# Two searches instead of one: where blocks 6 and 7 of the indexer are scored and selected

## The chip, the cores and the metric

The kernel runs on one core of one Trainium2 chip. The metric is the device time of one execution in microseconds (us). The engines are called PE (TensorE), DVE (VectorE), ACT (ScalarE), POOL (GpSimd) and SP (SyncE, which here issues all the DMAs). Each engine takes its instructions in order; between engines, semaphores make them wait.

## What is computed

A trunk of two layers over 1024 tokens of width 1024. Layer 0 has sparse latent attention whose keys are chosen by an indexer, layer 1 has windowed attention; both read a memory by cross-attention, and both end in a gated MLP with a causal convolution. The change touches the indexer of layer 0, which for every block of 128 queries scores all earlier keys and keeps the best 256:

```python
def one_block(args):
    ql, qr, qi, wi, t = args
    dots = jnp.einsum('bqhd,bsd->bqhs', qi, k_idx).astype(jnp.float32)
    score = jnp.einsum('bqhs,bqh->bqs', jax.nn.relu(dots), wi.astype(jnp.float32))
    score = jnp.where((key_pos[None, :] <= t[:, None])[None], score, -jnp.inf)
    _, idx = lax.top_k(score, topk)          # topk = 256
    c_sel = jax.vmap(lambda c, i: c[i])(c_kv, idx)
    ...                                      # softmax attention over the selected keys
    return jnp.einsum('bqhk,bqkr->bqhr', p, c_sel.astype(jnp.float32))
x = x + jnp.concatenate([mix, mem_o], axis=-1) @ w_out
x = x + conv_glu_ffn(rmsnorm(x, g_ffn[i]), f_w_up[i], f_conv_w[i], f_conv_b[i], f_w_down[i])
```

The indexer has 16 heads of width 64. Blocks 0 and 1 see at most 256 keys and need no selection.

## The kernel before

**Tiling.** The 1024 tokens are two halves of 512 and eight blocks of 128. A float32 product is made of three matmuls of high and low parts (`mm3`, lines 256 to 258); the high part of a weight is cast by ACT (line 99), its low part subtracted by POOL (line 279). PSUM holds four one-bank tiles (`pB`) and two two-bank tiles (`pS`). Nearly all else is in one pool of 51 tiles in SBUF (`t` in the rows).

**Order.** The program is written out by hand: PE's main stream calls `tick(ns)` after each few matmuls, and `tick` advances a planner's clock and the generators in `self.bg`. A generator yields the ns that its last step is meant to take, and goes on when its clock (the planner's times its rate) has caught up. So the rate and the yielded numbers set between which main instructions a background step is put, on every engine, and nothing else: matmuls of a background step don't advance the clock. `finish_bg` puts all that is left of a generator at one place.

**Stages of layer 0.** Projections; from 401 us the attention of the first half (`run_a(0)`), from 541 us its MLP (`ffn`), then attention and MLP of the second half. In the MLP, each of 22 hidden units has two projections of 24 matmuls into `pB` tiles; `conv` (lines 797 to 812) takes the first: DVE L801, ACT L802, DVE L803 and L804, ACT's Silu L810, POOL L811; then `gate` (DVE L816, ACT L820) takes the second. After each pair of units a down product makes four `pS` tiles of 12 matmuls, and each is added to the residual by DVE (L867).

**Scoring** (`indexer`, lines 1196 to 1227): a head of a block is four matmuls (L1214) into two `pB` tiles, two Relus on ACT (L1217) and a weighted add to the block's scores on DVE (L1222; the first head is L1220). Blocks 4 to 7 are 64 heads, scored during the projections at rate 0.65.

**Search** (`topk`, lines 1229 to 1322): the 256th best score of each query is found bit by bit, 32 bits. For blocks given in `act` ACT counts (a Sign with a running sum, L1274), for the others DVE counts (L1254); a step of two small DVE instructions (L1265, L1267) then sets the next bit. After the bits, blocks counted by ACT need a selection between two candidates (L1295 to L1304), and every block gets five passes that turn its scores into a mask (L1313 to L1321). Blocks 2 and 3 have a search of their own. Blocks 4 to 7 share one: DVE counts 4 and 5, ACT counts 6 and 7, and a bit is four yields of 2400 ns. It is the background entry `late`, at rate 1.0 in the first attention, 0 in its last products, 1.056 in the MLP. The masks of blocks 4 to 7 are first needed by the attention of the second half. The cross-attention of the memory for the second half (`memory()`: L713, then L752) starts when `late` is done.

Of the kernel before, what the change touches and what calls it, by code (L numbers as in the profile page):

```python
# [173 lines left out]
class Trunk:  # L174
# [1543 lines left out]
    def run(self):  # L1718
# [31 lines left out]
        def first_norms():  # L1750
            yield from self.scale_later(acc, rb, wait=8500)
            yield from self.norm_apply(rb[0], x0, g[:, 0], 2, h0, 1500)

        bn = self.add_bg(first_norms())
# [17 lines left out]
        def memory():  # L1772
            yield from self.mem_norm()
            yield from self.mem_kv(0)
            del self.mn

        self.a_qidx(0, h0, tabs[1])
        self.finish_bg(bn)
        bm = self.add_bg(memory(), 0.62)
        tabs = self.load_table("small", 1), self.load_table("q16", 1)  # L1780

        def index():
            yield 12864
            yield from self.indexer((2, 3))
            bt.append(self.add_bg(self.topk((2, 3), 1400, (3,))))
            while "qi1" not in self.marks:
                yield 500
            yield 9000
            be[1] = 0.65
            yield from self.indexer((4, 5, 6, 7))  # L1790
            late.append(self.add_bg(self.topk((4, 5, 6, 7), 2400, (6, 7))))

        late = []
        bt = []
        be = self.add_bg(index(), 1.0)
        self.finish_bg(b1)
        del x1
# [12 lines left out]
        late = late[0]  # L1810
# [7 lines left out]
        late[1] = 1.0  # L1818
        mem_o = mem[1]

        def topk_on():
            late[1] = 1.056
            yield 0

        for hf in range(2):
            x = self.load_x(a["x"][hf])
            sqs, h, hook = self.prepare(x, g[:, 3])
            last = self.run_a(hf, att, x, mem_o, bm, hook)
            late[1] = 0.0
            self.every(last)  # L1830
            rb = []
            bn = self.add_bg(self.chain([lambda: self.scale_of(sqs, rb, 1000), topk_on]))
            acc, hook = self.squares(x)
            if hf == 0:
                mem = self.mem_units(1)

                def memory():
                    while late in self.bg:
                        yield 1000
                    self.load_qmem(1)  # L1840
                    yield 9000
                    yield from self.whole(mem[0], 2200)

                def then():
                    nonlocal att
                    att = self.attn_a(1)
                    bt.append(self.add_bg(self.spread(self.chain([lambda: iter([4000]), lambda: self.begin_a(att)]), 2950)))

                bm, bt = self.add_bg(memory()), []
            else:  # L1850
                hB0 = []

                def norm0():
                    yield 55000
                    x0 = self.load_x(self.x_d[0])
                    yield from self.norm(x0, g[:, 1], hB0, 5000, 6000, 4000, True)

                b0 = self.add_bg(norm0())

                def mem_kv():  # L1860
                    yield 120000
                    yield from self.mem_norm()
                    yield 3000
                    yield from self.mem_kv(1)
                    del self.mn

                bt = [self.add_bg(mem_kv(), 0.8)]
            self.ffn(0, [(hf, x, h, rb, hook)], then=then if hf == 0 else None)
            self.finish_bg(bn, late, *bt)
            if hf == 0:  # L1870
                self.add_bg(self.store_x(x, self.x_d[0]))
                mem_o = mem[1]
# [284 lines left out]
```

## Time and profile before

| | us |
|---|---|
| median of 3 runs (2631.11 to 2632.77) | 2632.64 |
| the profiled execution | 2624.22 |
| its span | 2622.4 |
| PE busy | 2457.8 (94%) |
| DVE busy | 1708.0 (65%) |
| POOL busy | 1387.8 (53%) |
| ACT busy | 1207.9 (46%) |

A busy time is the time in which the engine has an instruction at work; a full PE can still be slow, since its granted clock (PEclk, a share of full speed) falls. The averages mix stages with different limits, so the rows below go by stretches of the span.

### The profile page before, as it was taken

The numbers are of one execution on the slowest core, as the hardware profiler recorded it, in microseconds if no ns is written. First come the engines' busy times: TensorE is split into PE (matmuls) and PEld (weight loads), VectorE is DVE, ScalarE is ACT, GpSimd is POOL, SyncE is SP. The second block draws the span as 40 slices with busy tenths as digits, with TensorE's granted clock in tenths as the row PEclk, the third lists the DMA queues.
The fourth block names the chain that finished last, engine by engine and source line by source line (L and its number), as shares of the span: only waits on it lengthen the run. The fifth ranks groups of instructions, "written<-read, shape, count | busy, mean of one in ns | idle before, by whom it ended". The sixth has DMA issues, their size and how long they took to land. (4 is left out here: it accounts for less than half of the span.)

```text
span 2622.4 us, 34006 instructions
## 1 busy us (share of the span) xinstructions
PE 2457.8 (94%) x11912; PEld 2053.0 (78%) x11912; DVE 1708.0 (65%) x2961; ACT 1207.9 (46%) x2270; POOL 1387.8 (53%) x1241
## 2 busy tenths in 40 slices
PE   7789978989998999999999989999989999999997
PEld 5678856878886888877888878878767888888886
DVE  7787788877688466665653353498786556564446
ACT  5355666655542555433333334588644444442003
POOL 5644223456665633365766665566656666664204
PEclk9899999999998999999999999999989999999999
DMA  5453343423322343322333345642254232348401
GB/s 202 148 172 120 127 159 135 149 78 97 98 87 91 126 155 107 113 97 82 105 127 97 99 115 187 213 139 88 81 193 137 104 122 97 123 170 329 142 16 65
DMA packets 121083, 333.83 MB, mean 127 GB/s; under 512 B 13008, under 2 KB 29904, under 8 KB 120912
## 3 DMA queue, kind: packets, MB, share of 16 engines
q1 hardware_dynamic: 120912, 331.66, 37.4%
q8 instruction: 94, 1.54, 0.2%
q14 instruction: 77, 0.63, 0.1%
HBM read 258.21 MB, written 73.40 MB: 126 GB/s over the span
## 5 line engine op out<-in xcount | busy, mean ns | idle before, releaser
L279 POOL TENSOR_TENSOR t<-t,t 128x512 fp32r<-128x512 f32 x829 | 1108.2, 1368 | 681.0 <-ACT t L99 273.6
L256 PE MATMUL pB<-t,t 128*128 128x512 f32 (+3 forms) x1824 | 682.1, 374 | 11.9 <-DVE t L781 4.1
L257 PE MATMUL pB<-t,t 128*128 128x512 f32 (+3 forms) x1824 | 678.8, 372 | 5.0 <-DVE t L461 2.4
L258 PE MATMUL pB<-t,t 128*128 128x512 f32 (+3 forms) x1824 | 678.3, 372 | 5.4 <-POOL t L279 5.4
L256 PE MATMUL pS<-t,t 128*128 128x512 f32 (+1 forms) x1460 | 573.8, 393 | 40.0 <-ACT t L99 19.1
L258 PE MATMUL pS<-t,t 128*128 128x512 f32 (+1 forms) x1460 | 568.5, 389 | 8.0 <-POOL t L279 7.8
L257 PE MATMUL pS<-t,t 128*128 128x512 f32 (+1 forms) x1460 | 568.0, 389 | 2.1 <-DVE t L512 2.1
L256 PEld LDWEIGHTS pB<-t,t 128*128 128x128 f32 (+1 forms) x1824 | 346.2, 190 | 72.8 <-DVE t L781 4.7
L258 PEld LDWEIGHTS pB<-t,t 128*128 128x128 f32 (+1 forms) x1824 | 345.9, 190 | 66.7 <-POOL t L279 6.7
L257 PEld LDWEIGHTS pB<-t,t 128*128 128x128 f32 (+1 forms) x1824 | 346.2, 190 | 64.7 <-DVE t L461 3.3
L256 PEld LDWEIGHTS pS<-t,t 128*128 128x128 f32 x1460 | 281.7, 193 | 100.4 <-ACT t L99 22.8
L99 ACT CAST t<-t 128x1024 fp32r<-128x1024 f32 x284 | 288.0, 1043 | 101.5 <-PE pS L258 44.1
L258 PEld LDWEIGHTS pS<-t,t 128*128 128x128 f32 x1460 | 281.0, 192 | 67.4 <-POOL t L279 12.1
L257 PEld LDWEIGHTS pS<-t,t 128*128 128x128 f32 x1460 | 281.8, 193 | 53.2 <-DVE t L512 2.5
L265 DVE TENSOR_TENSOR t<-pB,t 128x512 fp32r<-128x512 f32 (+3 forms) x248 | 149.8, 623 | 85.3 <-ACT t L264 82.7
L264 ACT CAST t<-pB 128x512 fp32r<-128x512 f32 (+3 forms) x248 | 125.7, 534 | 158.1 <-PE pB L258 96.2
L1055 DVE TENSOR_TENSOR t<-t,pS 128x1024 f32<-128x1024 f32 (+1 forms) x92 | 107.9, 1174 | 125.6 <-PE pS L258 125.5
L811 POOL TENSOR_TENSOR t<-t,t 128x512 f32<-128x512 f32 x44 | 57.5, 1306 | 161.6 <-ACT t L810 161.6
L867 DVE TENSOR_TENSOR t<-t,pS 128x1024 f32<-128x1024 f32 x88 | 106.8, 1217 | 53.0 <-PE pS L258 52.7
L1274 ACT ACTIVATE sign<-t,ti 128x1024 bf16<-128x1024 f32 (+1 forms) x96 | 96.5, 1005 | 60.5 <-DVE ti L1267 49.1
L1447 POOL TENSOR_SCALAR t<-t,st 128x128 f32<-128x128 f32 (+3 forms) x64 | 47.9, 750 | 141.3 <-DVE st L1446 88.0
L1222 DVE SCALAR_TENSOR_TENSOR t<-t,wtok,t 128x384 f32<-128x384 f32 (+5 forms) x90 | 97.0, 1077 | 24.5 <-ACT t L1217 20.7
(228 smaller groups left out, 3027.6 us busy)
## 6 DMA issues: line engine op xcount, KB each, us to landing
t<-in_up SPq DMA_DIRECT2D x138, 512.0 KB
t<-in_down SPq DMA_DIRECT2D x66, 512.0 KB
G_d<-t SPq DMA_DIRECT2D x44, 512.0 KB
t<-G_d SPq DMA_DIRECT2D x44, 512.0 KB
t<-in_a_in SPq DMA_DIRECT2D x34, 512.0 KB
t<-in_b_in SPq DMA_DIRECT2D x28, 512.0 KB
t<-in_a_out SPq DMA_DIRECT2D x20, 512.0 KB
t<-x_d SPq DMA_DIRECT2D x20, 512.0 KB
```

What stands on the lines that cost most here:

```text
L99: nc.scalar.copy(hi[:, :w], raw[:, :w])
L256: mm(out, a[0], b[0], start=start, stop=False, skip_group_check=again)
L257: mm(out, a[0], b[1], start=False, stop=False, skip_group_check=again)
L258: mm(out, a[1], b[0], start=False, stop=stop, skip_group_check=again)
L264: nc.scalar.copy(hi, src)
L265: nc.vector.tensor_tensor(lo, src, hi.bitcast(F32), op=OP.subtract)
L279: self.nc.gpsimd.tensor_tensor(lo[:, s], src[:, s], hi[:, s].bitcast(F32), op=OP.subtract)
L811: nc.gpsimd.tensor_tensor(v, v, rb[0], op=OP.mult)
L867: nc.vector.tensor_tensor(x[dp][:, :, t], x[dp][:, :, t], S, op=OP.add)
L1055: nc.vector.tensor_tensor(xp, xp, S, op=OP.add)
L1222: nc.vector.scalar_tensor_tensor(work[:, :n], tmp[:, :n], wv, work[:, :n], op0=OP.mult, op1=OP.add)
L1274: nc.scalar.activation(hits("sign")[:, :wide], self.work[blks[i]][:, :wide], AF.Sign, bias=cand[:, i:i + 1].bitcast(F32), accum_out=cnt[:, ...
```

## The change

The shared search of blocks 4 to 7 becomes two. During the projections only blocks 4 and 5 are scored, and their search (all counts on DVE, three yields of 2400 ns for a bit) starts when that is done. When the MLP of the first half has its norm, this search's rate becomes 0.8, and a new background entry starts: `later()` scores blocks 6 and 7 at rate 0.4 and then searches them at rate 1.0, all counts on ACT, three yields of 1650 ns for a bit. The cross-attention of the memory waits for both, and `finish_bg` at the MLP's end takes both.

```diff
--- before.py
+++ after.py
@@ -1787,8 +1787,8 @@
                 yield 500
             yield 9000
             be[1] = 0.65
-            yield from self.indexer((4, 5, 6, 7))
-            late.append(self.add_bg(self.topk((4, 5, 6, 7), 2400, (6, 7))))
+            yield from self.indexer((4, 5))
+            late.append(self.add_bg(self.topk((4, 5), 2400)))
 
         late = []
         bt = []
@@ -1818,9 +1818,18 @@
         late[1] = 1.0
         mem_o = mem[1]
 
+        def later():
+            yield from self.indexer((6, 7))
+            lates[1][1] = 1.0
+            yield from self.topk((6, 7), 1650, (6, 7))
+
         def topk_on():
-            late[1] = 1.056
+            late[1] = 0.8
+            if len(lates) == 1:
+                lates.append(self.add_bg(later(), 0.4))
             yield 0
+
+        lates = [late]
 
         for hf in range(2):
             x = self.load_x(a["x"][hf])
@@ -1835,7 +1844,7 @@
                 mem = self.mem_units(1)
 
                 def memory():
-                    while late in self.bg:
+                    while len(lates) < 2 or any(b in self.bg for b in lates):
                         yield 1000
                     self.load_qmem(1)
                     yield 9000
@@ -1866,7 +1875,7 @@
 
                 bt = [self.add_bg(mem_kv(), 0.8)]
             self.ffn(0, [(hf, x, h, rb, hook)], then=then if hf == 0 else None)
-            self.finish_bg(bn, late, *bt)
+            self.finish_bg(bn, *lates, *bt)
             if hf == 0:
                 self.add_bg(self.store_x(x, self.x_d[0]))
                 mem_o = mem[1]
```

PE during the projections (`pS` tiles of the queries' projection, `pB` of the scores; the tile numbers name t_2448, the index queries). One piece of the difference:

```order
 L257 MATMUL pS<-t_441,t_2241 128x512
 L258 MATMUL pS<-t_439,t_2242 128x512
-L1214 MATMUL pB<-t_834,t_2448 128x512
-L1214 MATMUL pB<-t_834,t_2448 128x384
-L1214 MATMUL pB<-t_835,t_2448 128x512
-L1214 MATMUL pB<-t_835,t_2448 128x384
 L256 MATMUL pS<-t_443,t_2241 128x512
 L257 MATMUL pS<-t_445,t_2241 128x512
```

One head of block 6, four matmuls, has left this place; 32 such heads do.

ACT at the sixth unit of the first half's MLP, before (t_2634 and t_3029 are the scores of blocks 6 and 7):

```order
L99 CAST t_5780<-t_5647 128x1024
L802 ACTIVATE t_5785<-t_5785,conv 128x512
L806 COPY prev_a<-t_5785 128x2
L810 ACTIVATE t_5785<-t_5785 128x512
L1274 ACTIVATE sign,tc<-t_2634,ti 128x1024
L820 CAST t_5736<-t_5785 128x512
L99 CAST t_5829<-t_5689 128x1024
L99 CAST t_5836<-t_5740 128x1024
L1274 ACTIVATE sign,tc<-t_3029,ti 128x1024
L1274 ACTIVATE sign,tc<-t_2634,ti 128x1024
L1274 ACTIVATE sign,tc<-t_3029,ti 128x1024
L99 CAST t_5915<-t_5778 128x1024
```

And the same place now (t_5585, t_5625 and the like at L1217 are each the Relu output of one head):

```order
L99 CAST t_5599<-t_5422 128x1024
L802 ACTIVATE t_5604<-t_5604,conv 128x512
L806 COPY prev_a<-t_5604 128x2
L810 ACTIVATE t_5604<-t_5604 128x512
L1217 ACTIVATE t_5625<-pB 128x512 x2
L1217 ACTIVATE t_5655<-pB 128x512 x2
L820 CAST t_5537<-t_5604 128x512
L99 CAST t_5664<-t_5468 128x1024
L99 CAST t_5671<-t_5541 128x1024
L1217 ACTIVATE t_5697<-pB 128x512 x2
L1217 ACTIVATE t_5723<-pB 128x512 x2
L1217 ACTIVATE t_5749<-pB 128x512 x2
```

The signs are gone from here, and two Relus of each head have come, in pairs, directly behind the unit's Silu (L810) and its cast (L820).

DVE from the sixteenth unit of the MLP into the down product behind it, before (t_3567 and the others at L867 are the residual):

```order
L816 TENSOR_TENSOR t_7095<-t_7095,pB 128x512
L1297 ISA t_7118,tc<-t_7118,t_3029 128x1024
L1297 ISA tc 128x1
L867 TENSOR_TENSOR t_3567<-t_3567,pS 128x1024
L1301 TENSOR_SCALAR ti<-tc 128x1
L1302 TENSOR_TENSOR ti<-tc 128x1
L1303 TENSOR_TENSOR ti<-ti 128x1
L1304 TENSOR_TENSOR ti<-ti,tc 128x1
L1254 TENSOR_SCALAR hit,tc<-t_3029,ti 128x1024
L867 TENSOR_TENSOR t_3569<-t_3569,pS 128x1024
L1308 TENSOR_SCALAR tc<-tc 128x4
L1313 TENSOR_SCALAR t_7194<-t_1911,ti 128x640
```

DVE from the twentieth unit into the down product behind it, now (t_5020 and t_5519 are the scores of blocks 6 and 7):

```order
L1254 TENSOR_SCALAR hit,tc<-t_5519,ti 128x1024
L1308 TENSOR_SCALAR tc<-tc 128x2
L1313 TENSOR_SCALAR t_7598<-t_5020,ti 128x896
L1315 SCALAR_TENSOR_TENSOR t_7599<-t_7598 128x896
L1317 SCALAR_TENSOR_TENSOR t_7599<-t_7599,tc,t_7598 128x896
L816 TENSOR_TENSOR t_7568<-t_7568,pB 128x512
L1319 SCALAR_TENSOR_TENSOR t_5020<-t_5020,ti,t_7599 128x896
L867 TENSOR_TENSOR t_3257<-t_3257,pS 128x1024
L1321 TENSOR_SCALAR t_5020<-t_5020 128x896
L1313 TENSOR_SCALAR t_7649<-t_5519,ti 128x1024
L1315 SCALAR_TENSOR_TENSOR t_7650<-t_7649 128x1024
L867 TENSOR_TENSOR t_3259<-t_3259,pS 128x1024
```

The end of the search of blocks 6 and 7 has moved by four units, the passes of blocks 4 and 5 are no longer in it, and passes of 6 and 7 stand ahead of the first residual add.

## Rows read from the trace of the kernel before

**Rows 1.** Busy time by stretch: us, busy time (instructions) of each engine, PEclk, DMA share, GB/s
```profile
200.00:340.00 140.00, 139.44 (x658) 115.80 (x657) 107.93 (x216) 85.19 (x187) 38.48 (x30) 1.00 0.37 120
...
340.00:363.00 23.00, 20.82 (x92) 14.80 (x90) 19.50 (x25) 15.14 (x27) 6.45 (x7) 1.00 0.53 166
...
378.00:401.00 23.00, 0.34 (x1) 0.34 (x2) 21.48 (x58) 5.70 (x15) 2.93 (x2) 0.55 0.36 129
...
401.00:430.00 29.00, 23.76 (x155) 20.09 (x155) 21.25 (x57) 20.32 (x51) 7.31 (x13) 0.94 0.21 77
...
430.00:530.00 100.00, 100.00 (x572) 86.37 (x572) 85.48 (x215) 67.10 (x139) 43.35 (x48) 1.00 0.48 159
...
566.00:602.00 36.00, 33.48 (x142) 27.30 (x141) 27.93 (x43) 20.70 (x32) 26.21 (x21) 0.95 0.27 88
...
602.00:765.00 163.00, 163.00 (x719) 134.66 (x718) 117.11 (x197) 87.63 (x134) 103.17 (x81) 1.00 0.29 97
...
765.00:850.00 85.00, 73.07 (x301) 58.17 (x301) 71.53 (x75) 23.30 (x37) 47.60 (x36) 0.90 0.24 81
```

**Rows 2.** Timeline of PE, last heads of scoring: start, us, instructions, idle before
```profile
347.35 1.20 PE L1214 MATMUL pB<-t,t 128*128 128x512 f32 x4 [0.23 <-ACT t L1217]
348.77 1.20 PE L1214 MATMUL pB<-t,t 128*128 128x512 f32 x4 [0.22 <-ACT t L1217]
```

**Rows 3.** Waits of PE, 400 to 530 us: us in total, times, longest
```profile
PE pB L713 <- DVE t L265: 22.8, 1, 22.8
```

**Rows 4.** Groups by shape, ACT, 602 to 765 us: busy us, mean ns, idle before
```profile
L1274 ACT ACTIVATE sign<-t,ti 128x1024 bf16<-128x1024 f32 x32 | 36.6, 1144 | 17.5 <-DVE ti L1267 17.2
...
L810 ACT ACTIVATE t<-t 128x512 f32<-128x512 f32 x10 | 6.3, 633 | 20.0 <-DVE ti L1265 12.4 <-DVE t L804 7.6
...
L1274 ACT ACTIVATION_READ_ACCUMULATOR sign<-t,ti 128x1 f32 x32 | 6.0, 187 | 0.0
```

**Rows 5.** Groups by shape, DVE, 602 to 765 us
```profile
L1267 DVE SCALAR_TENSOR_TENSOR ti<-ti 128x2 int32<-128x2 int32 x33 | 18.8, 569 | 1.1
...
L1265 DVE TENSOR_SCALAR ti<-tc 128x2 int32<-128x2 f32 x33 | 13.2, 400 | 0.1
```

**Rows 6.** Groups by shape, DVE, 200 to 345 us: scoring adds
```profile
L1222 DVE SCALAR_TENSOR_TENSOR t<-t,wtok,t 128x896 f32<-128x896 f32 x15 | 18.0, 1198 | 6.8 <-ACT t L1217 6.7
...
L1222 DVE SCALAR_TENSOR_TENSOR t<-t,wtok,t 128x1024 f32<-128x1024 f32 x7 | 9.0, 1283 | 5.4 <-ACT t L1217 5.4
```

**Rows 7.** Groups by shape, POOL, 602 to 765 us
```profile
L279 POOL TENSOR_TENSOR t<-t,t 128x512 fp32r<-128x512 f32 x71 | 90.6, 1310 | 31.6 <-ACT t L820 15.4 <-issue 11.5 <-ACT t L99 3.5
```

**Rows 8.** Timeline of DVE, 570 to 600 us
```profile
580.37 1.90 DVE L803 SCALAR_TENSOR_TENSOR t<-t,conv 128x511 f32<-128x511 f32 x1 [2.76 <-ACT t L802]
...
582.30 1.66 DVE L804 SCALAR_TENSOR_TENSOR t<-t,conv 128x510 f32<-128x510 f32 x1
...
587.89 1.22 DVE L867 TENSOR_TENSOR t<-t,pS 128x1024 f32<-128x1024 f32 x1
```

**Rows 9.** Timeline of DVE, 740 to 848 us
```profile
745.14 0.75 DVE L803 SCALAR_TENSOR_TENSOR t<-t,conv 128x511 f32<-128x511 f32 x1 [0.95 <-ACT t L802]
...
765.26 0.69 DVE L801 TENSOR_TENSOR t<-pB,t 128x512 f32<-128x512 f32 x1 [0.92 <-PE pB L258]
...
789.60 1.22 DVE L867 TENSOR_TENSOR t<-t,pS 128x1024 f32<-128x1024 f32 x1
...
818.07 2.07 DVE L1319 SCALAR_TENSOR_TENSOR t<-t,ti,t 128x896 f32<-128x896 f32 x1
...
821.98 2.28 DVE L1315 TENSOR_TENSOR_SCAN t<-t 128x1024 f32<-128x1024 f32 x1
```

**Rows 10.** Waits of PE, 545 to 765 us
```profile
PE pS L256 <- DVE t L867: 2.5, 1, 2.5
```

**Rows 11.** Waits of PE, 765 to 945 us
```profile
PE pS L258 <- POOL t L279: 5.3, 2, 3.1
...
PE pS L256 <- DVE ti L1301: 3.9, 1, 3.9
```

## The prediction

> **What bounds the kernel now.** I first read the busy time of every engine by stretch [rows 1], then the waits of PE, then the order in which instructions stand. PE is full wherever the change takes work from or brings work to: 139.4 of 140 us in the stretch of projections at 200 to 340 us, 100 of 100 at 430 to 530 (first attention), 163 of 163 at 602 to 765 (the first half's MLP) [rows 1]. No matmul is removed, so only idle time of PE and its slow matmuls can be won or lost. Between 340 and 850 us they lie in these places: 2.2 us at 340 to 363, the block at 378 to 401 in which PE does next to nothing, 5.2 us at 401 to 430, 2.5 us at 566 to 602 and 11.9 us at 765 to 850, with PEclk down to 0.55, 0.95 and 0.90 [rows 1]. The last one costs more than its idle time: at the 0.227 us per matmul of 602 to 765 (163 us, 719 of them) its 301 matmuls need 68.2 of 85 us, so 16.8 us are lost there.
>
> **The change, part by part**, against the profiled run (2624.2 us; the median of the runs is 8.4 us above it, so I add the difference to the median).
>
> Scoring blocks 6 and 7 is 32 heads of four matmuls, two Relus on ACT and one scaled add on DVE. Four matmuls take 4 x 0.227 = 0.91 us of a busy PE, so 29 us leave a full stretch and return in another full stretch: 0. What was wasted around them is won: the last seven heads stood alone, 1.42 us from start to start (347.35 to 348.77) instead of 0.91 [rows 2]. The whole idle time there is 2.2 us [rows 1]; I take **-2** (0 to -4).
>
> The block at 378 to 401 is PE waiting once, 22.8 us, for DVE to finish the search of blocks 2 and 3 [rows 3]. By the order the same nine counts, twelve steps and the tail of that search stand there afterwards: **0** (-2 to +2).
>
> In the first attention the search of 4 and 5 now counts two blocks every 7200 ns of the planner's clock, not every 9600, and the signs of 6 and 7 are gone from ACT. DVE is at 85.5 of 100 us there and PE is full [rows 1], so there is no stall to win but the 5.2 us at 401 to 430, where the memory attention's second part runs: **-1** (-5 to +4).
>
> The scoring in the MLP is the largest term. The stretch at 602 to 765 holds ten units (the ten Silus, L810) [rows 4], so a pair with its down product is 32.6 us, with 23.4 us of DVE. By the order one head comes to every 13 other matmuls, so 11 to a pair: 32.6 + 11 x 0.91 = 42.6 us. DVE has one step less for each bit (0.40 + 0.57 us [rows 5], 3.2 bits to a pair: -3.1) and 11 adds of 1.20 to 1.28 us, as they took during the projections [rows 6]: 23.4 - 3.1 + 13.6 = 33.9 us, 80% against 72% before. But the adds move beside a busy POOL (103 of 163 us, in pieces of 1.31 us [rows 1, 7]; 38.5 of 140 before [rows 1]). The conv's adds, which read two tiles in SBUF as these do, show what that does: the same L803 took 0.75 us at 745 us and 1.90 at 580 [rows 8, 9]. At 0.4 us more for each, DVE is at 38.3 of 42.6 us, 90%. The trace shows what follows from crowding: at 580 to 584 two such adds ran 1.90 and 1.66 us, the residual add L867 came at 587.89, and PE waited 2.5 us for it [rows 8, 10] and then ran at a lower clock (0.95 over 566 to 602 [rows 1]), about 3 us in all. ACT adds to it: a Relu stands behind the Silu, which waits for DVE, and the next head but one wants the Relu's PSUM bank; DVE's add waits for the Relu, and L867 stands behind that. Three down products fall into the scoring. The old stall of 3 us is in the first of them, so it goes (**-3**); against it I set somewhat less than one such stall for each, **+7**. Below, the adds hide at 80% of DVE (0); above, two stalls for each (+18).
>
> A rule of the Trainium skill bears on this. SBUF — State Buffer, section "Who interferes with whom": VectorE and GpSimd share a pair of ports, and a VectorE instruction with two SBUF inputs is blocked for the whole of a GpSimd instruction that reads SBUF. That speaks against moving these adds under the MLP's POOL work; the two L803 agree with it, and no row shows it for the scoring adds yet. By it each add could lose up to a whole 1.31 us, and if it did not hold for them the +7 would be about +2.
>
> Then the search of 6 and 7: 4950 ns of the planner's clock for a bit, where it was 9600 at rate 1.056. The 32 signs at 602 to 765 are 3.2 bits to a pair [rows 4]; now 5.9. ACT: 17.5 us a pair [rows 1] + 2.7 x 2 x (1.144 + 0.187) = 24.7 of 32.6. ACT takes its work in order, so waits count too: 2.0 us before each Silu and 1.1 us before the first sign of each bit, for DVE's step (20.0 us for ten, 17.5 for 16) [rows 4]. That is 4.0 + 6.5 more: 35.2 us, 2.6 over a pair, 14 us over the 5.4 pairs. Much of it falls together when ACT runs late, and at 54% of ACT nothing stalled. Where ACT is late, DVE's step waits for the sign and L867 stands behind it. I take **+4** (0 to +14).
>
> The end of the searches is all DVE: selections (L1295 to L1304), then five passes for each block. In the old place PE waited 3.9 us at the selection and 5.3 at the passes [rows 11] and lost 16.8 in all. It is now in two pieces. Blocks 4 and 5: ten passes beside one down product, some 1.4 us too much for each of two residual adds; about +3. Blocks 6 and 7: before, 24.3 us passed from the conv (L801) to the first residual add (L867) [rows 9]. By the order block 6's selection and a count (7.6 us) now stand ahead of that conv, while block 7's small steps, a count and block 6's passes (11.1 us) come before the add: 27.9 us, by the 56 rows from 765.26 to 818.07, of which the first and the last stand in [rows 9]. So PE waits some 3.6 us longer at that add, and passes such as the 2.28 us scan behind it [rows 9] crowd three more adds, about 5 us; but the four tails' 5.3 us of waiting are gone, and some of the slow matmuls behind them. Together **+2** (-8 to +8).
>
> The second memory attention waits for both searches; its second part goes from the MLP into the second attention. The same part cost up to 5.2 us in the first attention [rows 1] and about nothing in the MLP: **+2** (-1 to +5).
>
> Sum: -2 - 1 - 3 + 7 + 4 + 2 + 2 = **+9 us**, 2641.6.
>
> **The rivals.** (a) Faster: scoring hides as the counts did at 602 to 765, and two shorter ends overload DVE less than one long one, since four PSUM banks and two residual tiles each time absorb a few us. Then -2 - 1 - 3 + 1 + 0 - 7 + 0 = -12: 2621. For it: PE held 163 of 163 with DVE at 72%. Against: 80 to 90% is more, and DVE's work in the tail is the same. It decides whether DVE keeps L867 within a PSUM tile's 2.7 us. (b) Even: +4 for the scoring, +1 for the search, 0 for the tail, +1 for the memory, less 6: 2633. (c) Much slower: ACT is the bound of the dense search, in order behind DVE: +14 there and +14 in the scoring, +4 for the rest, less 6: 2659. (d) The search doesn't end before the MLP does and drains with PE idle. By the order it ends some 260 matmuls ahead, so this can hardly be; it would be slower too.
>
> **How the numbers follow.** Forecast 0.36 (2638 to 2650), (a) 0.19, (b) 0.27, (c) 0.16, (d) 0.02. A measurement of this kernel tells 0.2% apart, 5.3 us: faster (under 2627.4) is (a), 0.19; same is (b), 0.27; slower is the rest, 0.54. For 8 in 10 the range takes in most of (a) and (c): 2622 to 2662.
>
> **What would show it.** Right: in the profile after, PE waits on L867 and on the Relus' banks in the scoring stretch, at DVE 85% or more and adds of 1.5 us; waits of DVE for signs; the block at 378 us, about 29 us earlier, unchanged. The forecast is wrong if PE is full through the scoring and the dense search, or if the two ends together lose clearly less than 16.8 us.

## The result

The changed kernel takes **2669.51 us** (median of four runs, 2667.5 to 2673.6) against 2631.88 us for the kernel before on the same chip: 1.0156 times, 95% interval 1.0140 to 1.0171. It is slower by 1.6%, 37.6 us. The forecast was 2641.6 us with a range up to 2662: the direction was right, the size was not, and the time lies above the range. The profiled execution took 2670.62 us, with a span of 2668.4 us.

**Where the time went.** First the line of busy times of both pages, before and then after:

```profile
PE 2457.8 (94%) x11912; PEld 2053.0 (78%) x11912; DVE 1708.0 (65%) x2961; ACT 1207.9 (46%) x2270; POOL 1387.8 (53%) x1241
```
```profile
PE 2474.6 (93%) x11912; PEld 2067.4 (77%) x11912; DVE 1708.2 (64%) x2963; ACT 1205.2 (45%) x2266; POOL 1392.7 (52%) x1241
```

The same 11912 matmuls keep PE busy 16.8 us longer: slower matmuls, since the granted clock fell (mean PEclk 0.973 before, 0.964 after). The span is 46.0 us longer, so the other 29.2 us are idle time of PE. DVE, ACT and POOL do what they did. So the change made no work; it made PE wait, and clock was lost with the waits.

Next the stretches of the kernel after, in the columns of [rows 1]: the block at the end of the search of 2 and 3, the first attention, the scoring of blocks 6 and 7, their search, and the end of that search.

```profile
344.00:368.00 24.00, 1.38 (x7) 0.90 (x6) 21.70 (x61) 6.50 (x15) 2.93 (x2) 0.58 0.48 177
395.00:500.00 105.00, 104.45 (x593) 90.04 (x592) 93.03 (x223) 53.60 (x113) 43.97 (x49) 1.00 0.48 160
514.00:683.00 169.00, 150.37 (x629) 122.02 (x628) 116.36 (x156) 76.91 (x130) 79.29 (x57) 0.94 0.25 75
683.00:880.00 197.00, 176.17 (x734) 142.64 (x733) 105.92 (x151) 119.18 (x187) 107.07 (x82) 0.94 0.24 78
880.00:921.00 41.00, 33.56 (x137) 26.80 (x136) 37.55 (x42) 9.99 (x14) 26.69 (x16) 0.92 0.31 100
```

Where PE held 163 of 163 us before [rows 1], it now holds 150.4 of 169 and 176.2 of 197, at 0.94 of the clock. And no other engine is full in these two: DVE stands at 69% and 54%, ACT at 46% and 60%. That is the main thing to see: **no engine is full by its busy time, and yet PE waits.**

Between the same instructions in both traces, after less before: from the start of the kernel to the end of the first attention -34.3 us, of which 29.1 are the scoring that left the projections; from there to the MLP's first conv -0.9; then to the conv at which scoring ends 169.5 us for 118.1, **+22.3** over the 29.1 that came; from there to the conv at which the search ends 196.3 for 183.0, **+13.3**, though the kernel before lost its 16.8 us of [rows 1] inside that stretch; the rest of the MLP +0.5; the second attention 194.3 for 184.0, +10.3; and -0.5 up to the second MLP's down products. That is 39.8. The last 6.2 us come in code that the change doesn't touch, and the profiled run of before was 8 us under its median; I don't put them down to the change.

The waits of PE in the scoring (510 to 680 us), then in the search (680 to 935 us), in the columns of [rows 3]:

```profile
PE pS L256 <- DVE t L867: 11.4, 3, 7.5
PE pB L1214 <- ACT t L1217: 7.2, 5, 2.7
```
```profile
PE pS L256 <- DVE t L867: 28.3, 9, 6.2
```

Before, the residual add L867 was waited for once in 220 us [rows 10]. Now it is the thing most waited for. Why it is late stands in DVE's groups by shape, first in the scoring, then (L1265) in the search; the last column is the idle time ahead of the instruction and who ended it:

```profile
L1222 DVE SCALAR_TENSOR_TENSOR t<-t,wtok,t 128x1024 f32<-128x1024 f32 x15 | 23.4, 1557 | 20.7 <-ACT t L1217 20.7
L1222 DVE SCALAR_TENSOR_TENSOR t<-t,wtok,t 128x896 f32<-128x896 f32 x15 | 22.0, 1470 | 13.3 <-ACT t L1217 13.3
```
```profile
L1265 DVE TENSOR_SCALAR ti<-tc 128x2 int32<-128x2 f32 x31 | 12.2, 394 | 41.4 <-ACT sign L1274 41.4
```

DVE stands idle for 34 us in front of scoring adds, for the Relu, and for 41 us in front of search steps, for the sign. Before, the step waited 0.1 us in all [rows 5].

The longest stall, 7.5 us, shows the chain. ACT, then DVE, then PE, each a timeline (start, us, instruction, idle before):

```profile
660.68 0.62 ACT L820 CAST t<-t 128x512 fp32r<-128x512 f32 x1 [3.04 <-DVE t L816]
661.20 1.99 ACT L99 CAST t<-t 128x1024 fp32r<-128x1024 f32 x2
663.10 1.07 ACT L1217 ACTIVATE t<-pB 128x512 f32<-128x512 f32 x2
```
```profile
659.97 0.68 DVE L816 TENSOR_TENSOR t<-t,pB 128x512 f32<-128x512 f32 x1
664.21 1.98 DVE L1222 SCALAR_TENSOR_TENSOR t<-t,wtok,t 128x1024 f32<-128x1024 f32 x1 [3.56 <-ACT t L1217]
666.11 1.22 DVE L1265 TENSOR_SCALAR ti<-tc 128x2 int32<-128x2 f32 x1
667.37 1.18 DVE L1267 SCALAR_TENSOR_TENSOR ti<-ti 128x2 int32<-128x2 int32 x1
668.47 1.21 DVE L867 TENSOR_TENSOR t<-t,pS 128x1024 f32<-128x1024 f32 x1
```
```profile
661.64 0.39 PE L257 MATMUL pS<-t,t 128*128 128x512 f32 x1
661.87 0.39 PE L258 MATMUL pS<-t,t 128*128 128x512 f32 x1
669.73 0.79 PE L256 MATMUL pS<-t,t 128*128 128x512 f32 x1 [7.47 <-DVE t L867]
670.32 0.63 PE L257 MATMUL pS<-t,t 128*128 128x512 f32 x1
670.75 0.63 PE L258 MATMUL pS<-t,t 128*128 128x512 f32 x1
```

DVE's gate L816 frees ACT's cast L820; two weight casts L99 stand behind it, the head's Relus behind those. DVE's add waits 3.56 us for them, and a step of the search of 4 and 5 and then L867, whose product had been ready since about 659.5, stand behind the add. PE fills the other two-bank tile until 662.3; the next one it needs is the one that L867 has to empty. Before the wait matmuls start 0.23 us apart, after it 0.43: the granted clock is 0.50 from 669.7 to 675.3 us, where 13 matmuls take 5.6 us in place of 3.0.

In the search the same chain has the sign in the Relu's place. One stall of it, of 3.96 us, ends at 755.24 us (its PE line is among the four below e5). ACT, then DVE:

```profile
747.64 1.99 ACT L99 CAST t<-t 128x1024 fp32r<-128x1024 f32 x2
```
```profile
752.09 0.76 DVE L1265 TENSOR_SCALAR ti<-tc 128x2 int32<-128x2 f32 x1 [3.87 <-ACT sign L1274]
752.88 1.18 DVE L1267 SCALAR_TENSOR_TENSOR ti<-ti 128x2 int32<-128x2 int32 x1
753.98 2.34 DVE L867 TENSOR_TENSOR t<-t,pS 128x1024 f32<-128x1024 f32 x2
```

Two weight casts stand ahead of the bit's two signs, DVE's step waits for the signs, and L867 stands behind the step.

### The profile page after: what moved, and what is told of

It reads as the page before. It is cut to its first block, busy times and chain, and to the rows that moved or that the text cites. A ratio compares the mean times of both kernels' runs of the same rounds, so it can differ in the third digit from the quotient of the medians.

```text
span 2668.4 us, 33982 instructions
## 1 busy us (share of the span) xinstructions
PE 2474.6 (93%) x11912; PEld 2067.4 (77%) x11912; DVE 1708.2 (64%) x2963; ACT 1205.2 (45%) x2266; POOL 1392.7 (52%) x1241
## 5 line engine op out<-in xcount | busy, mean ns | idle before, releaser
L99 ACT CAST t<-t 128x1024 fp32r<-128x1024 f32 x284 | 288.6, 1043 | 101.3 <-PE pS L258 49.5
L867 DVE TENSOR_TENSOR t<-t,pS 128x1024 f32<-128x1024 f32 x88 | 106.5, 1215 | 57.0 <-PE pS L258 57.0
L1222 DVE SCALAR_TENSOR_TENSOR t<-t,wtok,t 128x384 f32<-128x384 f32 (+5 forms) x90 | 104.3, 1158 | 45.5 <-ACT t L1217 42.7
```

The source lines that it names most:

```text
L99: nc.scalar.copy(hi[:, :w], raw[:, :w])
L867: nc.vector.tensor_tensor(x[dp][:, :, t], x[dp][:, :, t], S, op=OP.add)
L1222: nc.vector.scalar_tensor_tensor(work[:, :n], tmp[:, :n], wv, work[:, :n], op0=OP.mult, op1=OP.add)
```

## The experiments

**Theory.** The scoring loses because DVE's add waits in order for a Relu that is late on ACT; the search loses because DVE's step waits in order for the sign (and the next sign for the step); in both, L867 stands behind the waiting instruction. **Rivals.** DVE and its port are too full (the adds grew from 1.20 and 1.28 us [rows 6] to 1.47 and 1.56); the `pB` banks run out (7.2 us at L1214); ACT has too much to do; two searches cost more than one whatever their pace. Ratios below are against the kernel before, run on the same chip beside each.

**e1 and e2: the scoring back in the projections, at two paces.**

```diff
-            yield from self.indexer((4, 5))
+            yield from self.indexer((4, 5, 6, 7))
...
-            yield from self.indexer((6, 7))
             lates[1][1] = 1.0
+            yield 0
             yield from self.topk((6, 7), 1650, (6, 7))
```

That is e1; e2 has 2400 for 1650 in the last line as well.

> Blocks 6 and 7 are scored in the second half's projections again, as in the kernel before; their search stays a search of their own at pace 1650, started where the scoring would now start minus its time, and blocks 4 and 5 keep theirs. Waiting theory (the scoring in the MLP costs 22 us net, because VectorE's add waits in order for the Relu, that Relu stands behind casts and Silu on ScalarE, and L867 stands behind the add): about 2645 us, 20 to 27 under the changed kernel, and about 13 over the kernel before for the dense search that is left; VectorE idle before L1222 for L1217 small again in the projections, as before the change. Rival (the loss is that of a dense search of two blocks on ScalarE, and the scoring costs the 4 us of the forecast): 2662 to 2667 us.

> As the run before (blocks 6 and 7 scored in the projections), and the search of blocks 6 and 7 with its steps 2400 ns apart in place of 1650, over the same stretch that the search of 4 to 7 took in the kernel before. Waiting theory: the idle time of L1265 for L1274's sign falls from 41 us to under 12, TensorE loses as little there as before the change, 2632 us, 2624 to 2640. Rival (splitting the search in two costs in itself, whatever its pace, since each of its steps is a chain of sign and two 128x1 operations): no less than the run before it, about 2645 us.

e1: 2668.4 us, 1.0154 (1.0139 to 1.0170). e2: 2629.81 us, 1.0005 (0.9996 to 1.0015). e2's time came as the waiting theory said: two searches in place of one cost nothing, and the rival on that is out. (The step's idle time did not fall under the 12 us expected; it is 23 us, and costs next to nothing there.) e1 was a **miss**: undoing the scoring's move gave back nothing. DVE's step in both, 555 to 870 us, e1 and then e2:

```profile
L1265 DVE TENSOR_SCALAR ti<-tc 128x2 int32<-128x2 f32 x50 | 16.7, 335 | 39.8 <-ACT sign L1274 39.7
```
```profile
L1265 DVE TENSOR_SCALAR ti<-tc 128x2 int32<-128x2 f32 x50 | 21.1, 423 | 23.2 <-ACT sign L1274 22.9
```

and PE's waits for L867 there, e1 and then e2:

```profile
PE pS L256 <- DVE t L867: 32.0, 9, 10.8
```
```profile
PE pS L256 <- DVE t L867: 8.7, 6, 1.9
```

Without the scoring the search of 6 and 7 begins at 557 us and not at 670, and so runs at 1650 ns beside the last 18 bits of the search of 4 and 5, which lasts to 749 us, and not only beside its end. From the first to the twenty-fifth L867 e1 loses 45 us on the kernel before. So, as I read it, e1 didn't take one cause away alone; it put more of the other in its place. It does show that the pace alone, with no scoring in the MLP, can cost all that the change cost: e1 and e2 differ by one number and by 38.6 us.

**e3: the add of blocks 6 and 7 one head later.**

```diff
+        late = []
...
-                if hd == 0:
...
+                def add(hd=hd, wv=wv, tmp=tmp, work=work, n=n):
+                    if hd == 0:
...
+                late.append(add)
+                del tmp
+                if len(late) > (1 if blk > 5 else 0):
+                    late.pop(0)()
                 yield 1.05 * n + 100
             if g:
+                while late:
+                    late.pop(0)()
```

> The changed kernel, with the add of blocks 6 and 7's scoring (L1222) written one head later, after the next head's Relus; the same instructions in number, nothing left out. Waiting theory: VectorE's idle time before L1222 falls from 34 us in the scoring to under 8, TensorE's waits for L867 there from 11 us to under 5, and the time by 10 to 18 us, to 2652 to 2660. Rival (VectorE and its port are simply too full in the scoring: the adds took 1.47 and 1.56 us for 1.20 and 1.28): within 3 us of the changed kernel, 2667 to 2672, since the add is as long as before wherever it stands. Rival (the Relu's bank pB, not the add, holds the projection): no gain either, and L1214's waits for L1217 stay at 7 us.

Measured: 2649.14 us, 1.0078 (1.0061 to 1.0095), 20.4 us under the changed kernel and somewhat more than the 10 to 18 expected. The add is now L1225, the Relu L1218. DVE's adds, PE's waits (514 to 655 us) and the stretch of the scoring:

```profile
L1225 DVE SCALAR_TENSOR_TENSOR t<-t,wtok,t 128x1024 f32<-128x1024 f32 x15 | 22.6, 1505 | 1.2 <-ACT t L1218 1.2
L1225 DVE SCALAR_TENSOR_TENSOR t<-t,wtok,t 128x896 f32<-128x896 f32 x15 | 20.9, 1394 | 0.4 <-ACT t L1218 0.4
```
```profile
PE pB L1215 <- ACT t L1218: 3.1, 3, 2.7
PE pS L256 <- DVE t L867: 1.5, 1, 1.5
```
```profile
516.00:653.00 137.00, 132.38 (x587) 109.08 (x586) 114.88 (x138) 68.01 (x117) 80.62 (x53) 1.00 0.26 81
```

The idle time before the add falls from 34 to 1.6 us, PE runs at full clock, and the last matmul of the scoring comes at 646 us and not at 658. From the MLP's first conv to the ninth it takes 149.0 us, where the changed kernel took 169.6; the kernel before took 118.1, which with the 29.1 of moved work is 147.2. The adds are almost as long as in the changed kernel, 1.39 and 1.51 us: their length, and with it the port, costs at most the 1.8 us that are left; DVE is at 84% and has room, and ACT, which does the same work as before the edit, was not too full. The theory holds for the scoring. The wait for the banks was more than halved without any more of them, so more than half of it came from the same lateness.

**e4: both signs of a bit one behind the other, the step two paces after them.**

```diff
-                yield pace
+                yield pace if own else 2 * pace * k
```

> The changed kernel, with the two signs of a bit written back to back and VectorE's step 3300 ns after them in place of 1650, in the search of blocks 6 and 7 alone; the same instructions in the same whole time. Waiting theory: L1265's idle time for L1274 falls from 41 us to under 15, TensorE's waits for L867 between 680 and 935 us from 28 to under 12, the time by 8 to 14 us, to 2656 to 2662. Rival (ScalarE in order: the signs of 1.1 us hold the casts of the MLP, and their order within a bit is no matter): within 3 us of the changed kernel, or up to 5 slower, since two signs in a row hold a cast for 2.3 us.

Measured: 2659.73 us, 1.0117 (1.0098 to 1.0137): 9.8 us under the changed kernel, as expected. The step (672 to 925 us) and PE (676 to 935 us):

```profile
L1265 DVE TENSOR_SCALAR ti<-tc 128x2 int32<-128x2 f32 x34 | 12.7, 373 | 29.8 <-ACT sign L1274 29.8
```
```profile
PE pS L256 <- DVE t L867: 21.2, 8, 6.7
```

The step still waits 29.8 us, not under 15, and PE 21.2 us, not under 12. Half right: order within a bit matters, but 3300 ns of the planner's clock behind the second sign isn't always enough for ACT to be done with it.

**e5: the ring of sign and step cut.** Signs of the search of 6 and 7 take a fixed bias, its steps read a fixed count; every instruction stands where it stood, and two small memsets are added. What this search finds is no threshold.

```diff
+        fix = self.sb.tile([128, 4], F32, name="tf", tag="tf", bufs=2) if act and not own else None
+        if fix is not None:
+            nc.vector.memset(fix[:, 0:2], -1e9)
+            nc.vector.memset(fix[:, 2:4], 1e9)
...
-            nc.vector.tensor_scalar(drop[:, at], cnt[:, at], float(need), float(1 << bit) if bit < 31 else -1.0,
+            had = cnt[:, at] if fix is None else fix[:, 0:2] if bit == 31 else fix[:, 2:4]
+            nc.vector.tensor_scalar(drop[:, at], had, float(need), float(1 << bit) if bit < 31 else -1.0,
...
-                                         bias=cand[:, i:i + 1].bitcast(F32), accum_out=cnt[:, i:i + 1])
+                                         bias=cand[:, i:i + 1].bitcast(F32) if fix is None else fix[:, 2:3],
+                                         accum_out=cnt[:, i:i + 1])
```

> The changed kernel, in which the search of blocks 6 and 7 runs with the same instructions at the same places, but its signs take a fixed bias and VectorE's two steps of a bit read a fixed count, so that neither engine waits for the other there; what it finds for blocks 6 and 7 is therefore no threshold (their selection is left out in effect). The scoring is untouched. Waiting theory (the dense search loses by the ring sign, step, sign between two queues in order): L1265's idle time for L1274 goes from 42 us to 0, TensorE's waits for L867 after 680 us fall from 28 to under 10, PE's busy time falls as its clock comes back, and the time by 15 to 22 us, to 2647 to 2655. Rival (load: 64 signs of 1.1 us and 64 pairs of steps are too many for ScalarE and VectorE in that stretch, waits or none): 2660 to 2670 us.

Measured: 2646.14 us, 1.0064 (1.0049 to 1.0078), **23.4 us** under the changed kernel; the waits for L867 came out a little above the 10 us expected. The steps of this search (510 to 950 us) and PE's waits (680 to 925 us):

```profile
L1270 DVE TENSOR_SCALAR ti<-tf 128x2 int32<-128x2 f32 x32 | 13.7, 429 | 0.0
```
```profile
PE pS L256 <- DVE t L867: 12.1, 4, 5.9
```

In the changed kernel PE's timeline has these stalls between 744 and 840 us, far from either search's end:

```profile
748.27 0.50 PE L256 MATMUL pS<-t,t 128*128 128x512 f32 x1 [1.51 <-DVE t L867]
755.24 0.80 PE L256 MATMUL pS<-t,t 128*128 128x512 f32 x1 [3.96 <-DVE t L867]
794.68 0.75 PE L256 MATMUL pS<-t,t 128*128 128x512 f32 x1 [3.30 <-DVE t L867]
832.40 0.79 PE L256 MATMUL pS<-t,t 128*128 128x512 f32 x1 [5.89 <-DVE t L867]
```

None of the four is left in e5 (its profiled execution took 2641.1 us); its stalls over 1 us after 680 stand at the two ends of the searches, at about 702, 709, 871 and 883 us. And PE's busy time, with as many matmuls, is 2461.7 us in e5 for 2474.6: of the 29.1 us between the two spans 14.7 are those four stalls and 12.9 the clock. ACT still does all 64 signs at the same places, and DVE's steps are no shorter (429 ns for 394), so their load is not the cause of these 23 us; the waiting is.

**e6: e3 and e4 together.** The diff is that of both.

> The changed kernel with the later add and the later step together. If the two waits are causes of their own, their gains add: 2669.5 less 20 (late add) less 10 (late step), about 2639 us, 2635 to 2644. Rival (both gains are the same time, won back from one clock that the stalls hold down): 2645 us or more.

Measured: 2640.98 us, 1.0039 (1.0025 to 1.0053), 28.5 us under the changed kernel: the gains add up, so the two waits are causes of their own. PE busy 2459.1 us; the clock, 0.972, is that of before.

**e7, e8, e9: is the idle block before the first attention a matter of that search's pace?** The search of 2 and 3 was left alone by the change; its block [rows 3] is the largest stall of PE between the projections and the second MLP, in both kernels. Its pace becomes 1200 ns in e7, on e6, and in e8, on e2:

```diff
-            bt.append(self.add_bg(self.topk((2, 3), 1400, (3,))))
+            bt.append(self.add_bg(self.topk((2, 3), 1200, (3,))))
```

e9 is e8 with 1000.

> As the run before it, with the search of blocks 2 and 3 (in the second half's projections) at a step of 1200 ns in place of 1400, so that it ends some 19 us earlier: 32 bits by 3 steps by 200 ns. The idle stretch of 22.6 us of TensorE before the first attention falls under 8 us if the search has no other limit; 12 to 18 under the run before it, about 2624 us. Rival (that search is bound by ScalarE's and VectorE's order already, as the dense search of 6 and 7 was): the idle stretch falls by less than 5 us or the projections grow by what it loses, 2636 to 2645.

> The kernel of e2 (blocks 6 and 7 scored in the projections, their search at 2400 ns, 2629.8 us) with the search of blocks 2 and 3 at 1200 ns in place of 1400. Theory: the idle stretch of 22.6 us at 375 us falls under 8 us, 2612 to 2619 us, under the kernel before by 0.4 to 0.6 per cent. Rival (a denser search of 2 and 3 waits in the projections as that of 6 and 7 did in the MLP): 2628 to 2636 us.

> The kernel of e8 with the search of blocks 2 and 3 at 1000 ns in place of 1200. From 1400 to 1200 its last sign came 10 us earlier and TensorE's idle stretch fell from 22.6 to 15.9 us, the rest of which is the end of that search (from its first L1304 to its last scan). Theory: another 10 to 19 us earlier, the end lies in the projections too, the stretch falls under 5 us, and the time by 8 to 14 under e8's 2626.5, to 2612 to 2618 us. Rival (VectorE is too full in the projections, so what the stretch gives the projections take): 2623 to 2630 us.

Measured: e7 2636.1 us, 1.0022 (1.0012 to 1.0032); e8 2626.46 us, 0.9988 (0.9978 to 0.9997); e9 2631.93 us, 1.0010 (1.0000 to 1.0021). The gains expected, 8 to 18 us at each, were misses. At 360 to 410 us PE's waits, e8 and then e9:

```profile
PE pB L713 <- DVE t L265: 15.9, 1, 15.9
```
```profile
PE pB L256 <- DVE t L265: 5.3, 1, 5.3
PE pB L713 <- DVE t L265: 3.3, 1, 3.3
```

The block does shrink, from 22.6 us to 15.9 and 8.6. Of the first 6.7 us some 4.5 reach the time, by the ratios, in e7 against e6 as in e8 against e2; of the next 7.3 none (e9 is slower than e8). The projections ahead of it, 220 to 360 us, e8 and then e9:

```profile
220.00:360.00 140.00, 135.34 (x631) 110.34 (x630) 116.12 (x232) 90.73 (x200) 31.17 (x26) 1.00 0.39 125
```
```profile
220.00:360.00 140.00, 132.13 (x605) 106.50 (x603) 117.67 (x252) 85.81 (x190) 33.07 (x26) 0.99 0.32 107
```

The search at 1000 ns makes PE wait there (26 fewer matmuls by 360 us), and both kernels begin the norm ahead of the MLP within 0.3 us of each other, at 525.8 and 526.0 us, for 529.0 in e2. The rival holds in full from 1200 to 1000 ns, and in part from 1400 to 1200: what the block gives, the projections take.

**e10 and e12: the late step on e9 and on e8.** The diff is that of e4.

> The kernel of e9 with the step of the search of blocks 6 and 7 late, as in e4 (both signs of a bit back to back, the step 4800 ns after them). Waiting theory: L1265's idle time for L1274, 23 us in e2, falls under 12, and the time by 3 to 6 us under e9's. Rival (at 2400 ns the waits already fit in VectorE's slack): within 2 us of e9.

> The kernel of e8 (2626.5 us) with the late step in the search of blocks 6 and 7 at 2400 ns. e9 and e10, which differ by the late step alone, stood within 1 us at every stage of their profiled executions, though their medians were 6 us apart. If the step is worth nothing at 2400 ns: 2625 to 2628 us, as e8. If the 6 us were the step's: 2619 to 2622 us.

Measured: e10 2625.9 us, 0.9990 (0.9981 to 0.9998); e12 **2620.88 us, 0.9974 (0.9962 to 0.9987)**. e12 is the best kernel that ran, a quarter of a per cent under the kernel before. By the ratios e10 is some 5 us under e9, and e12 some 4 under e8, the latter within the intervals. The step's idle time before the sign (540 to 860 us) falls as expected, from 22.9 us in e2 and e9 to 7.5 in e10 and e12. Where the time comes back is not settled: the profiled executions of e9 and e10 stand within 2.3 us of each other at the MLP's first conv and 1.2 at the first residual add of the second MLP, though e9's was 5 us quicker than its median; and e12's MLP has PE waiting 9.5 us for L867 where e2's had 10.3.

**e11: memory attention back in the MLP, on e6.**

```diff
-                    while len(lates) < 2 or any(b in self.bg for b in lates):
+                    while len(lates) < 2 or late in self.bg:
```

> The kernel of e6 (late add and late step, 2641.0 us), in which memory attention of the second half waits for the search of blocks 4 and 5 alone, as it stands some 180 us earlier in the MLP, and not for that of 6 and 7. Theory (the last 10 us over the kernel before are memory attention's second part, which falls into the second attention: 5 us of its own work there and as much in waits): 2634 to 2638 us, the stretch from the end of the MLP to the end of the second attention as long as before the change (184.0 us, against 194.3 after it). Rival (beside the dense search it takes VectorE's time just where that search is short of it): no gain, 2640 to 2646 us, the MLP longer by what the attention is shorter.

Measured: 2652.92 us, 1.0090 (1.0076 to 1.0104), 12 us over e6. From the last L867 of the MLP to the norm behind the second attention it takes 188.6 us for e6's 200.9, but the down products before it, from the first L867 to the last, 398.5 for 377.8. PE's waits at 750 to 800 us, where it now runs:

```profile
PE pB L752 <- DVE t L265: 4.4, 3, 2.4
PE pB L752 <- ACT t L264: 2.5, 1, 2.5
PE pB L738 <- ACT t L719: 2.4, 1, 2.4
```

The rival holds. The second attention is the better place for it; the change's wait for both searches is no part of the loss worth undoing.

## The prediction, step by step

**What bounds it.** Right that PE was full wherever work came from or went to, and that only idle time and slow matmuls could change. (Its list of idle places leaves out 4.9 us at 541 us, ahead of the MLP; they are there after, too, at 507.) The step that no term priced as such is the second half of that sentence: 16.8 of the 46.0 us came as slower matmuls behind the stalls. The forecast counted 3 us for a stall of 2.5 [rows 10]; in e5 four stalls of 14.7 us went together with 12.9 us of slower matmuls.

**The small terms.** The projections' end gained 3.9 us beyond the moved work (forecast 2, at most 4), the block at 378 us was 22.8 and is 22.6, 33 us earlier (forecast 0, and 29 earlier), the first attention and what leads to the MLP gained 2 us (forecast 1). These steps held.

**Scoring in the MLP, +7, bounds 0 to 18.** This step failed in size: it cost about 20 us, which is what e3 gives back, above its own upper bound. The mechanism was named (a Relu behind the Silu, the add behind the Relu, L867 behind the add), but the price was worked out from DVE's busy share and from the port, as one stall for each down product. DVE was to be 90% busy; it was 69% busy and idle for 34 us in front of the adds. With those waits gone, in e3, it is 84% busy and PE hardly waits: the load was not far off, the lateness was the missing term. The rows to go by were there: even in the projections, with ACT at 61% and no Silu or gate ahead, adds waited 12.2 us for their Relus in 22 adds [rows 6], 0.55 us each; in the MLP it was 1.13 us each. That the old stall at 586 us would go (-3) cannot be told apart from this: the MLP's first stalls over 2 us are now those on the Relu's bank.

**On the port** the added time of an add was 0.27 us, the forecast 0.4, and e3 says that it was hidden. The Trainium skill, SBUF — State Buffer, section "Who interferes with whom", has a VectorE instruction with two SBUF inputs contend with a GpSimd instruction that reads SBUF, and whichever comes second wait for the whole of the first. The trace agrees in kind: of the adds of 128x896, seven began with POOL at rest and took 1.14 to 1.15 us, and eight began inside an instruction of POOL's and took 1.42 to 2.29. Over the 30 adds, though, the mean cost of 0.27 us is a fifth of the 1.31 us of one such instruction.

**The dense search, +4, bounds 0 to 14.** This step failed in size too: 23.4 us, which is what e5 gives back. The prediction summed ACT's busy time and known waits to 35.2 us of a 32.6 us pair and then took +4, since much of it "falls together". ACT was 60% busy in fact. What decided was the ring: a step can't start before the signs, the next signs can't start before the step, and each waits its turn on an engine that may stand behind something else. In [rows 4] the sign already waited 17.2 us for the step at 9600 ns a bit, while the step waited 0.1 for the sign [rows 5]; at 4950 ns the slack that kept the latter at zero was used up, as I read it. The step's wait alone is not the loss: at 7200 ns a bit, in e2, it is 23 us and the time is that of before. It costs when L867 stands behind it and PE has no tile left. Rival (c) named this place, with ACT as the bound and +14 for each term: the nearest of the cases, right in its place, wrong in the bound (ACT was never full) and some 10 us short.

**The ends of the searches, +2.** Within its bounds. In the search's stretch the kernel after loses some 30 us (13.3 and the 16.8 that were there); 23 of them are the ring's, which leaves some 7 for the end of the search of 4 and 5. The rest of the MLP took 0.5 us more, though the memory attention's second part had left it: the second attention's PE busy time grew by 6.7 us (186.84 for 180.16). So the end of 6 and 7 lost about 7. Some 14 in all, for 16.8 before: about 3 us less where 2 more were forecast, a figure from differences that no run tests.

**Memory in the second attention, +2.** Its 10.3 us there are 6.7 of moved work and 3.6 of waiting; within its bounds, and e11 shows that the other place is dearer.

**The sum.** With 20.4 and 23.4 in place of 7 and 4 the same terms give 2632.6 + 9 + 32.8 = 2674 us, for 2669.5 measured. By this sum the miss is in those two terms. Rivals (a) and (b) fell with them, (d) did not happen: the last pass of the search began at 918 us, the last L867 at 969. Of the signs that the prediction gave for being right, the waits for L867, for the Relus' banks and for signs, the adds of 1.5 us and the unchanged block came; DVE at 85% or more in the scoring did not.

## What to carry to other kernels

When background work moves beside another stage, price it by chains and not by busy shares: for each new instruction that reads another engine's result, ask what stands ahead of the producer in its queue and what stands behind the consumer in its own; here two engines at 46 to 69% lost some 40 us to each other. The cure adds no instruction: write the consumer one piece of work later (the late add gave 20 us, the late step 10), and give a loop that goes back and forth between two queues a pace that leaves room for their lateness (2400 ns for 1650 gave 38.6 us between e1 and e2). With both cures the moved scoring is still 0.4% behind the kernel before (e6); the kernels that came out ahead of it score blocks 6 and 7 in the projections. A stall of PE is dearer than its length: in the two comparisons here 29.2 and 14.7 us of idle time came with 16.8 and 12.9 us of slower matmuls.

## What the runs showed of the hardware

An instruction of a step on 128x2 values took 0.16 us or 1.2 in the same kernel (L1265 at 746.12 and 666.11 us). This is the short one:

```profile
746.12 0.17 DVE L1265 TENSOR_SCALAR ti<-tc 128x2 int32<-128x2 f32 x1 [3.16 <-ACT sign L1274]
746.32 0.16 DVE L1267 SCALAR_TENSOR_TENSOR ti<-ti 128x2 int32<-128x2 int32 x1
```

and this is what POOL did in the two stretches:

```profile
743.76 1.30 POOL L811 TENSOR_TENSOR t<-t,t 128x512 f32<-128x512 f32 x1 [2.14 <-ACT t L810]
747.82 6.22 POOL L279 TENSOR_TENSOR t<-t,t 128x512 fp32r<-128x512 f32 x5 [2.76 <-ACT t L820]
```
```profile
661.37 7.15 POOL L279 TENSOR_TENSOR t<-t,t 128x512 fp32r<-128x512 f32 x5 [3.34 <-ACT t L820]
```

The short pair lies between two pieces of POOL's work, the long one (1.22 and 1.18 us, in the chain above) inside one. The two searches of the changed kernel have 64 such pairs. Of L1265, 37 began with POOL at rest and took 0.15 to 0.17 us; 27 began inside an instruction of POOL's and took up to 1.27, and 25 of these ended within 0.06 us of the end of an instruction of POOL's. Of L1267, 48 took 0.16 us and 16 began inside one and took 0.34 to 1.23; all 16 ended with one. So beside POOL a small DVE operation can cost as much as one of POOL's subtractions takes (1.37 us on average). The two long ones in the chain above are some 2 us of its 7.5. The forecast expected such waiting of the large adds alone; no run here took POOL's work away, so that it is POOL is read from the times, not tested.
